# Transposing attention probabilities on VectorE in 32x32 blocks instead of on TensorE

## The chip, the cores and the metric

The kernel runs on one core of a Trainium2 chip. The metric is the device time of one execution in microseconds (us). The core has engines that run beside each other, each through its own list of instructions in order: PE (TensorE, matrix products into PSUM), DVE (VectorE), ACT (ScalarE), POOL (GpSimd, unused here) and SP (SyncE, which here only issues the weight loads). An instruction waits, and everything behind it on its engine waits too, until the instructions of other engines that it depends on have finished.

## The reference

It is a two-layer decoder trunk over 256 tokens of width 2048, with 256 memory tokens. Layer 0 mixes tokens by trailing-window pooling, layer 1 by causal attention with 12 heads of 128; in both, 4 more heads attend to the memory tokens. With one block of 256 tokens the block-sparse attention is plain causal attention. Cut to what matters:

```python
for i in range(2):
    if i == 1: k, v = split(h @ w_kv_shared)               # 12 heads
    branch_in, gate_b, mem_q, gate_m = split(h @ w_in[i])
    branch = multiscale_pool(branch_in) if i == 0 else causal_attention(branch_in, k, v)
    mem_o = softmax(mem_q @ mk.T * 128**-0.5) @ mv         # 4 heads; mk, mv = split(mem @ w_mem_kv[i])
    mixed = concatenate([branch * silu(gate_b), mem_o * silu(gate_m)])
    h = layer_norm(alpha * h + mixed @ w_out[i])
```

Softmax runs over keys. The product with the values needs the probabilities with keys on the partitions, so they have to be transposed.

## The kernel before

Every matrix is streamed through the core in blocks of 128x1024 fp32 numbers (512 KB; `item`). A product is done at about fp32 precision with three products of rounded parts: `split` (L69) copies a block on ACT into a rounded high part (`wh`), and DVE subtracts it from the block to get the low part (`wl`). PE multiplies high by high, high by low and low by high, accumulating in PSUM (`acc`). One block feeds 16 matmuls in `proj_t` or 12 wider ones in `proj_n`.

`run` (L130) writes the order by hand. In the step of block i it emits, in this order, the `split` of block i+3 (`LP = 3`), the DMA load of block i+4 (`LD = 4`, issued by SP), the matmuls of block i (its `consume`), and then the events of step i. An event is a piece of other work that `later(n, fn)` (L92) has put n blocks behind the block at which it was planned. There are four buffers for `wh` and four for `wl` (`W_BUFS = 4`), so the split of block i+3 takes the buffer of block i-1 and can start when PE is through with that one.

Attention is done for two heads at a time: `MemPair` for memory heads, `MobaPair` for the 12 causal ones. Each layer has two memory pairs, layer 1 has six causal pairs (three groups of two): ten pairs in all. A pair has these pieces: `a` (PE computes the scores `s`, DVE the negated row maxima `nb`), `exps` (ACT: exponentials and row sums), `divide` (DVE: reciprocal and four scalings), `b(j)` for each head (PE transposes the probabilities `p` against `ident` into the PSUM tile `pt`, L312 and L362; ACT and DVE split `pt` into `ph`, `pl`), and `c` (PE multiplies by the values into `o`; `gated` multiplies by the gate on DVE and splits the result into `zT`, which the output projection reads). `plan(pr, a, b, c)` (L380) gives the blocks at which `a`, the first `b` and `c` stand, counted from the last query block of the pair's group; `exps` and `divide` stand one and two blocks after `a`, the second `b` one after the first. Below, "block n" is the n-th block after that last query block, and "block 0" is the query block itself.

Of the kernel before, what the change touches and what calls it, by code (L numbers as in the profile page):

```python
# [11 lines left out]
F32 = mybir.dt.float32  # L12
F32R = mybir.dt.float32r
AF = mybir.ActivationFunctionType
ALU = mybir.AluOpType
AX = mybir.AxisListType

P = 128
T = 256
# [13 lines left out]
BLK = 1024  # L33
RAW_BUFS = 4
WARM = 10
SHIFT = 40
W_BUFS = 4
SHIFT = 40
LD = 4
# [6 lines left out]
def trunk(ctx: ExitStack, tc: tile.TileContext, a: dict, out: bass.AP):  # L46
    nc = tc.nc
    ctx.enter_context(tc.manual_schedule())
    sb = ctx.enter_context(tc.tile_pool(name="sb", bufs=1))
    ps = ctx.enter_context(tc.tile_pool(name="ps", bufs=1, space=bass.MemoryType.PSUM))  # L50
# [7 lines left out]
    kept = [xm[:, i * KX:(i + 1) * KX].rearrange("p (k n) -> p k n", k=KT) for i in range(2)]  # L58
    zT = sb.tile([P, KT, 2 * T], F32R, name="zT")
    res = sb.tile([P, 2, D], F32, name="res")  # L60
    ident = mask = psc = eps_t = stats = None

    f = lambda ap: ap.bitcast(F32)

# [4 lines left out]
    def split(hi, lo, src):  # L69

        nc.scalar.activation(hi, src, AF.Copy)  # L71
        nc.vector.tensor_sub(lo, src, f(hi))  # L72
# [19 lines left out]
    def later(n, fn):  # L92
        events[now[0] + n].append(fn)
# [162 lines left out]
    class Rows:  # L256
# [17 lines left out]
        def divide(self):  # L274
            nc.vector.reciprocal(self.sm, self.sm)
            for c, (src, dst) in enumerate(self.rows):
                nc.vector.tensor_scalar_mul(dst, dst, self.sm[:, c:c + 1])

    def gated(o, g, kt):

        zf = sb.tile([P, T], F32, name="zf", bufs=3)
        nc.vector.scalar_tensor_tensor(zf, o, 0.5, g, op0=ALU.mult, op1=ALU.mult)  # L282
        split(zT[:, kt, :T], zT[:, kt, T:], zf)

    class MemPair(Rows):
        def __init__(self, h0, st):
# [2 lines left out]
        def a(self):  # L289
            q, k = self.st["q"], self.st["k"]  # L290
            s = ps.tile([P, 2, 2, T], F32, name="s2")
            for j in range(2):
                h = self.h0 + j
                for t in range(2):
                    qh = q[:, h, t * P:(t + 1) * P]
                    ql = q[:, h, T + t * P:T + (t + 1) * P]
                    mm(s[:, j, t], qh, k[:, h, :T], True, False)
                    mm(s[:, j, t], qh, k[:, h, T:], False, False)
                    mm(s[:, j, t], ql, k[:, h, :T], False, True)
            self.p = p = sb.tile([P, 2, 512], F32, name="p")  # L300
            p4 = p.rearrange("p j (t m) -> p j t m", t=2)
            self.rows = [(s[:, j, t], p4[:, j, t]) for j in range(2) for t in range(2)]
            self.maxima([(0, 4, s)])

        def b(self, j):
            if j == 0:
                self.ph = sb.tile([P, 2, 512], F32R, name="ph")
                self.pl = sb.tile([P, 2, 512], F32R, name="pl")
            pt = ps.tile([P, 512], F32, name="pt")
            for m in range(2):  # L310
                for t in range(2):
                    nc.tensor.transpose(pt[:, m * T + t * P:m * T + (t + 1) * P],  # L312
                                        self.p[:, j, t * T + m * P:t * T + (m + 1) * P], ident)
            split(self.ph[:, j], self.pl[:, j], pt)

        def c(self):
            v, g = self.st["v"], self.st["g"]
            o = ps.tile([P, 2, T], F32, name="o")
            for j in range(2):
                h = self.h0 + j  # L320
                for m in range(2):
                    vh = v[:, m, 0, h * HD:(h + 1) * HD]
                    vl = v[:, m, 1, h * HD:(h + 1) * HD]
                    s = slice(m * T, (m + 1) * T)
                    mm(o[:, j], vh, self.ph[:, j, s], m == 0, False)
                    mm(o[:, j], vh, self.pl[:, j, s], False, False)
                    mm(o[:, j], vl, self.ph[:, j, s], False, m == 1)
            for j in range(2):
                gated(o[:, j], g[:, self.h0 + j, :], 12 + self.h0 + j)

    class MobaPair(Rows):

# [4 lines left out]
        def a(self):  # L337
            q, k = self.st["q"], self.st["k"]
            s = ps.tile([P, 2, 512], F32, name="s2")
            for j in range(2):  # L340
                h = self.h0 + j
                for t, (c0, w) in enumerate(((0, P), (P, T))):
                    qh = q[:, h, t * P:(t + 1) * P]
                    ql = q[:, h, T + t * P:T + (t + 1) * P]
                    d = s[:, j, c0:c0 + w]
                    mm(d, qh, k[:, h, :w], True, False)
                    mm(d, qh, k[:, h, T:T + w], False, False)
                    mm(d, ql, k[:, h, :w], False, True)
            self.p = p = sb.tile([P, 2, 512], F32, name="p")
            nc.vector.tensor_tensor(p[:, :, :384], s[:, :, :384],  # L350
                                    mask[:, None, :].to_broadcast([P, 2, 384]), op=ALU.add)

            self.rows = [(p[:, j, c0:c1],) * 2 for c0, c1 in ((0, P), (P, 384)) for j in range(2)]
            self.maxima([(0, 2, p[:, :, :P]), (2, 4, p[:, :, P:384])])

        def b(self, j):
            if j == 0:
                self.ph = sb.tile([P, 2, 512], F32R, name="ph")
                self.pl = sb.tile([P, 2, 512], F32R, name="pl")
            pt = ps.tile([P, 512], F32, name="pt")  # L360
            for c in range(3):
                nc.tensor.transpose(pt[:, c * P:(c + 1) * P], self.p[:, j, c * P:(c + 1) * P], ident)  # L362
            split(self.ph[:, j, :384], self.pl[:, j, :384], pt[:, :384])

        def c(self):
            v, g = self.st["v"], self.st["g"]
            o = ps.tile([P, 2, T], F32, name="o")
            for j in range(2):
                h = self.h0 + j

                for m, (d, s) in enumerate(((o[:, j], slice(0, T)), (o[:, j, P:], slice(T, 384)))):
                    vh = v[:, m, 0, h * HD:(h + 1) * HD]
                    vl = v[:, m, 1, h * HD:(h + 1) * HD]
                    mm(d, vh, self.ph[:, j, s], m == 0, False)
                    mm(d, vh, self.pl[:, j, s], False, False)
                    mm(d, vl, self.ph[:, j, s], False, m == 1)
            for j in range(2):
                gated(o[:, j], g[:, self.h0 + j, :], self.kt0 + j)

    def plan(pr, a, b, c):  # L380

        later(a, pr.a)
        later(a + 1, pr.exps)
        later(a + 2, pr.divide)
        later(b, lambda: pr.b(0))
        later(b + 1, lambda: pr.b(1))
        later(c, pr.c)
# [21 lines left out]
    def load_gb(n):  # L409
        gb = []  # L410
        for nm in ("ln_g", "ln_b"):
            tl = sb.tile([P, 512], F32, name=nm, bufs=2)
            src = a[nm][0, n * 512:(n + 1) * 512]
            nc.sync.dma_start(tl, src[None, :].to_broadcast([P, 512]))
            gb.append(tl)
        return gb
# [13 lines left out]

    def constants():

        nonlocal ident, mask, psc, eps_t, stats
        ident = sb.tile([P, P], F32, name="ident")
        mask = sb.tile([P, 384], F32, name="mask")
        psc = sb.tile([P, 12], F32, name="psc")
        eps_t = sb.tile([P, 48], F32, name="eps_t")
        stats = sb.tile([P, 2, 5, 6], F32, name="stats")
        nc.vector.memset(eps_t[:, 0:1], EPS)
        nc.scalar.dma_start(ident, a["ident"])  # L440
        nc.scalar.dma_start(mask, a["mask"])
        for g in range(2):
            inv.append(sb.tile([P, 2, T], F32, name="ln_g", bufs=2))
            nc.scalar.dma_start(inv[g], a["inv"][None, 2 * g:2 * g + 2].to_broadcast([P, 2, T]))
        nc.scalar.dma_start(psc, a["pool_scale"])

        def prepare():
            nc.vector.tensor_scalar_mul(psc, psc, 0.5)
            for z in (U0, U1, S0, S1):
                nc.vector.memset(z[:, :, :PAD], 0.0)  # L450
        later(20, prepare)
# [44 lines left out]
    def mem_q_gate(layer):  # L496
        q = fresh("q", lambda: heads_tile("qq"))
        g = fresh("g", gate_tile)
        for c in range(2):
            proj_t(xT, w_in(layer, 12 + c), to_heads(q, 2 * c))  # L500
        prs = [MemPair(0, st), MemPair(2, st)]

        def go():
            plan(prs[0], 1, 5, 9)
            plan(prs[1], 7, 11, 14)
        after(go)
        for c in range(2):
            proj_t(xT, w_in(layer, 14 + c), to_gate(g, 2 * c))
# [98 lines left out]
    for half in range(2):  # L607
# [3 lines left out]
        g = fresh("g", gate_tile)  # L611
# [43 lines left out]
    for grp in range(3):  # L655
        k = fresh("k", lambda: heads_tile("kk"))
        q = fresh("q", lambda: heads_tile("qq"))
        g = fresh("g", gate_tile)
# [5 lines left out]
        prs = [MobaPair(2 * j, 4 * grp + 2 * j, st) for j in range(2)]  # L664

        def go(prs=prs):
            plan(prs[0], 1, 5, 17)
            plan(prs[1], 7, 18, 20)
        after(go)
        for c in range(2):  # L670
            proj_t(xT, w_in(1, 6 + 2 * grp + c), to_gate(g, 2 * c))
# [94 lines left out]
    o = last(0, 0, 512)  # L766
# [95 lines left out]
```

## Time and profile before

| what | value |
|---|---|
| median of 3 runs | 822.19 us (822.07 to 822.66) |
| profiled execution, its own time | 822.53 us |
| its span, first to last instruction | 820.8 us |
| PE busy | 810.8 us, 99% of the span |
| DVE busy | 558.5 us, 68% |
| ACT busy | 396.2 us, 48% |
| HBM traffic | 193 GB/s over the span |

The span is what the trace covers; 1.7 us of the execution's own time lie around it. Busy time of PE counts overlapping matmuls once, so a busy PE says that it had work, not how fast it worked. What a piece of PE's work costs is read from the chain of waits, in which each piece begins where the one before has ended.

### The profile page before, as it was taken

How to read it: one execution, taken by the hardware profiler on the slowest of the kernel's cores; microseconds unless marked ns; L12 is line 12 of the kernel's file. 1: busy time of each engine (PE TensorE's matmuls, PEld its weight loads, DVE VectorE, ACT ScalarE, POOL GpSimd, SP SyncE). 2: the span in 40 equal slices, each digit the busy share in tenths (PEclk: the TensorE clock that was granted, in tenths of full speed). 3: DMA queues.
4: the chain of work that ended last, by engine and by line, in shares of the span. 5: the costliest groups of instructions: out<-in, count | busy, mean ns of one | idle time of the engine just before them, and what ended most of it. 6: DMA issues, size and time to landing. Idle time of an engine off the chain costs nothing.

```text
span 820.8 us, 11537 instructions
## 1 busy us (share of the span) xinstructions
PE 810.8 (99%) x4446; PEld 700.9 (85%) x4446; DVE 558.5 (68%) x794; ACT 396.2 (48%) x578; POOL 0.2 (0%) x4
## 2 busy tenths in 40 slices
PE   9999999999999999999999999999999999999996
PEld 6888888898888888888888888888888888888885
DVE  5786678657956555797667667576765667658746
ACT  6564545545545343545455445354554445545520
POOL 0000000000000000000000000000000000000000
PEclk9999999999999999999999999999999999999998
DMA  8876545456557655676554544645455554636742
GB/s 319 298 250 206 170 154 192 172 181 212 185 190 278 221 186 199 201 234 201 185 170 143 193 162 163 212 159 189 177 173 170 185 187 158 224 113 233 277 132 103
DMA packets 47164, 159.15 MB, mean 194 GB/s; under 512 B 5375, under 2 KB 7167, under 8 KB 46847
## 3 DMA queue, kind: packets, MB, share of 16 engines
q1 hardware_dynamic: 45792, 155.21, 56.3%
q10 hardware_dynamic: 1316, 3.19, 1.0%
q8 instruction: 35, 0.57, 0.3%
q14 instruction: 21, 0.17, 0.1%
HBM read 156.28 MB, written 2.10 MB: 193 GB/s over the span
## 4 chain that ended last, share of the span: by engine, by line
PE 98%; DVE 1%; DMA 1%; SPq 0%; ACT 0%; issue 0%; DVEq 0%
PE acc L67 89%; PE o L67 4%; PE s L67 2%; PE pt L67 2%; DMA raw<-in_w_mk 1%; PE pt L362 0%; PE pt L312 0%; SPq L98 0%; DVE res L805 0%; PE o L637 0%; PE pt L637 0%; DVE res L786 0%; DVE wl L72 0%; ACT wh L71 0%; DVE stats L744 0%
## 5 line engine op out<-in xcount | busy, mean ns | idle before, releaser
L67 PE MATMUL acc<-xm,wh 128*128 128x512 f32 x1344 | 466.8, 394 | 0.5 <-ACT wh L71 0.5
L72 DVE TENSOR_TENSOR wl<-raw,wh 128x1024 fp32r<-128x1024 f32 (+2 forms) x250 | 295.0, 1187 | 149.8 <-ACT wh L71 148.8
L67 PE MATMUL acc<-xm,wl 128*128 128x256 f32 x1344 | 362.6, 280 | 0.1
L71 ACT ACTIVATE wh<-raw 128x1024 fp32r<-128x1024 f32 (+2 forms) x250 | 255.5, 1028 | 188.5 <-PE acc L67 131.2
L67 PEld LDWEIGHTS acc<-xm,wh 128*128 128x128 f32 x1344 | 247.2, 188 | 49.1 <-ACT wh L71 1.0
L67 PEld LDWEIGHTS acc<-xm,wl 128*128 128x128 f32 x1344 | 252.7, 188 | 7.9 <-DVE wl L72 0.9
L67 PE MATMUL acc<-wh,zT 128*128 128x512 f32 x448 | 140.0, 390 | 0.0
L67 PEld LDWEIGHTS acc<-wh,zT 128*128 128x128 f32 x448 | 84.1, 188 | 17.3
L67 PE MATMUL acc<-wl,zT 128*128 128x512 f32 x224 | 87.2, 389 | 0.0
L67 PE MATMUL acc<-xm 128*128 128x512 f32 x288 | 65.8, 389 | 0.0
L67 PEld LDWEIGHTS acc<-xm 128*128 128x128 f32 x288 | 54.1, 188 | 11.2
L72 DVE TENSOR_TENSOR xm<-raw,xm 128x1024 fp32r<-128x1024 f32 (+2 forms) x41 | 47.8, 1171 | 21.1 <-ACT xm L71 21.1
L220 ACT ACTIVATE fold<-acc 128x256 f32<-128x256 f32 x72 | 27.7, 385 | 60.8 <-PE acc L67 59.6
L71 ACT ACTIVATE xm<-raw 128x1024 fp32r<-128x1024 f32 (+2 forms) x41 | 41.3, 1014 | 19.1 <-PE acc L67 9.8
L67 PEld LDWEIGHTS acc<-wl,zT 128*128 128x128 f32 x224 | 42.1, 188 | 8.5
L221 DVE TENSOR_TENSOR fold<-acc,fold 128x256 f32<-128x256 f32 x72 | 29.5, 419 | 4.6 <-ACT fold L220 4.6
L71 ACT ACTIVATE zT<-zf 128x256 fp32r<-128x256 f32 x32 | 12.9, 414 | 39.6 <-DVE zf L282 35.4
L67 PE MATMUL acc<-xm,zT 128*128 128x256 f32 (+1 forms) x144 | 22.6, 318 | 0.0
L67 PEld LDWEIGHTS acc<-xm,zT 128*128 128x128 f32 x144 | 20.7, 190 | 1.9
L67 PE MATMUL acc<-wh,xm 128*128 128x512 f32 x64 | 21.6, 403 | 0.0
L71 ACT ACTIVATE ph<-pt 128x384 fp32r<-128x384 f32 (+1 forms) x20 | 10.7, 535 | 22.2 <-PE pt L362 13.5
L72 DVE TENSOR_TENSOR zT<-zf,zT 128x256 fp32r<-128x256 f32 x32 | 12.9, 423 | 9.7 <-ACT zT L71 9.7
(124 smaller groups left out, 504.4 us busy)
## 6 DMA issues: line engine op xcount, KB each, us to landing
raw<-in_w_in SPq DMA_DIRECT2D x128, 512.0 KB, 3.5
raw<-in_w_out SPq DMA_DIRECT2D x64, 512.0 KB, 4.1
raw<-in_w_sk SPq DMA_DIRECT2D x24, 512.0 KB, 4.4
raw<-in_w_sv SPq DMA_DIRECT2D x24, 512.0 KB, 3.3
raw<-in_w_mv SPq DMA_DIRECT2D x14, 512.0 KB, 5.2
raw<-in_w_mk SPq DMA_DIRECT2D x12, 512.0 KB, 3.4
raw<-in_xT SPq DMA_DIRECT2D x4, 512.0 KB, 4.8
res<-in_x ACTq DMA_DIRECT2D x2, 1024.0 KB, 5.4
```

The source lines that it names most:

```text
L67: nc.tensor.matmul(o, l, r, start=start, stop=stop)
L71: nc.scalar.activation(hi, src, AF.Copy)
L72: nc.vector.tensor_sub(lo, src, f(hi))
L220: nc.scalar.activation(dst, acc[:, T:], AF.Copy)
L221: nc.vector.tensor_add(dst, acc[:, :T], dst)
```

## The change

All 68 transposes on PE go. In their place DVE transposes the divided probabilities in blocks of 32x32 (`turn`): one instruction reads 32 partitions and writes 32 others, transposing each 32x32 block on the way; 16 instructions (four `turn` groups of four) do a pair. For that `exps` writes the exponentials into a new tile `ebuf`, with columns rearranged in pieces of 32, `divide` scales them there, `turn` writes into `p`, and `b` splits `p` instead of `pt`. `ebuf` is one tile for all pairs, and it takes the place of the two `ln_b` buffers of the first layer norm. `gated` does both heads' products first and then both splits. The plans change: the second pair's `a` stands one block later, `turn` groups stand between `divide` and `b`, and the `b` and `c` of memory pairs stand later, the second pair's `c` at block 23 instead of 14.

```diff
+        def blocks(self, n):
+            self.n = 32 * n
+            self.p = sb.tile([P, 2, 512], F32, name="p").rearrange("p j c -> p (j c)")
+            self.e = ebuf.rearrange("p j c -> p (j c)")[:, :4 * self.n]
...
+        def turn(self, *groups):
+            for g in groups:
+                for h in range(4):
+                    nc.vector.transpose(self.p[32 * g:32 * g + 32, h * self.n:(h + 1) * self.n],
+                                        self.e[32 * h:32 * h + 32, g * self.n:(g + 1) * self.n])
...
-        zf = sb.tile([P, T], F32, name="zf", bufs=3)
-        nc.vector.scalar_tensor_tensor(zf, o, 0.5, g, op0=ALU.mult, op1=ALU.mult)
-        split(zT[:, kt, :T], zT[:, kt, T:], zf)
+        zfs = [sb.tile([P, T], F32, name="zf", bufs=3) for _ in range(2)]
+        for j, zf in enumerate(zfs):
+            nc.vector.scalar_tensor_tensor(zf, o[:, j], 0.5, g[:, j], op0=ALU.mult, op1=ALU.mult)
+        for j, zf in enumerate(zfs):
+            split(zT[:, kt + j, :T], zT[:, kt + j, T:], zf)
...
-            pt = ps.tile([P, 512], F32, name="pt")
-            for m in range(2):
-                for t in range(2):
-                    nc.tensor.transpose(pt[:, m * T + t * P:m * T + (t + 1) * P],
-                                        self.p[:, j, t * T + m * P:t * T + (m + 1) * P], ident)
-            split(self.ph[:, j], self.pl[:, j], pt)
+            hi, lo = (t[:, j].rearrange("p (m h s) -> p m h s", m=4, h=4) for t in (self.ph, self.pl))
+            split(hi, lo, self.group(self.p, 4 * j, 4 * j + 4, 4))
...
-    def plan(pr, a, b, c):
+    def plan(pr, a, turns, b, c):
...
+        for g, t in enumerate(turns):
+            later(t, lambda g=g: pr.turn(g))
...
-            tl = sb.tile([P, 512], F32, name=nm, bufs=2)
+            tl = sb.tile([P, 512], F32, name=nm, bufs=2) if nm == "ln_g" else ebuf[:, n % 2]
...
-            plan(prs[0], 1, 5, 9)
-            plan(prs[1], 7, 11, 14)
+            plan(prs[0], 1, (4, 5, 6, 6), 7, 10)
+            plan(prs[1], 8, (11, 13, 16, 18), 20, 23)
...
-            plan(prs[0], 1, 5, 17)
-            plan(prs[1], 7, 18, 20)
+            plan(prs[0], 1, (4, 5, 5, 6), 7, 17)
+            plan(prs[1], 8, (11, 13, 14, 15), 18, 20)
```

The following shows DVE's list in layer 0 from block 14 to block 20 of the memory heads, where the pooling begins (`res` is scratch for the pooling there, its three-part rows are pooling steps of a group of 384 channels). Before:

```order
L282 SCALAR_TENSOR_TENSOR zf<-o,gate 128x256
L72 TENSOR_TENSOR zT<-zf,zT 128x256
L72 TENSOR_TENSOR wl<-raw,wh 128x1024 x2
L221 TENSOR_TENSOR res<-acc,res 128x256 x2
L541 TENSOR_TENSOR res<-res 128x3x256
L72 TENSOR_TENSOR wl<-raw,wh 128x1024
L549 TENSOR_TENSOR res<-res,ln_g 128x3x256
L72 TENSOR_TENSOR wl<-raw,wh 128x1024
L550 TENSOR_TENSOR res<-res 128x3x256
L72 TENSOR_TENSOR zT<-res,zT 128x3x256
L72 TENSOR_TENSOR wl<-raw,wh 128x1024 x2
```

And now:

```order
L294 STREAM_TRANSPOSE p<-ebuf 32x256 x4
L71 TENSOR_TENSOR wl<-raw,wh 128x1024 x3
L220 TENSOR_TENSOR res<-acc,res 128x256 x2
L294 STREAM_TRANSPOSE p<-ebuf 32x256 x4
L559 TENSOR_TENSOR res<-res 128x3x256
L71 TENSOR_TENSOR wl<-raw,wh 128x1024
L567 TENSOR_TENSOR res<-res,ln_g 128x3x256
L71 TENSOR_TENSOR wl<-raw,wh 128x1024
L294 STREAM_TRANSPOSE p<-ebuf 32x256 x4
L568 TENSOR_TENSOR res<-res 128x3x256
L71 TENSOR_TENSOR zT<-res,zT 128x3x256
L71 TENSOR_TENSOR wl<-raw,wh 128x1024 x2
```

Two groups of four transposes (blocks 16 and 18) now stand among the pooling steps, in front of the `wl` of block 22, which is the first of the two in the last row; the second pair's `gated` has left the head of the piece.

On DVE in the first group of causal heads, from block 4 to block 7 of the first pair (`xm` takes the low parts of the value blocks there). Before:

```order
L221 TENSOR_TENSOR fold<-acc,fold 128x256 x2
L72 TENSOR_TENSOR wl<-raw,wh 128x1024
L72 TENSOR_TENSOR pl<-pt,ph 128x384
L242 SCALAR_TENSOR_TENSOR gate<-th,fold 128x256 x2
L72 TENSOR_TENSOR xm<-raw,xm 128x1024
L72 TENSOR_TENSOR pl<-pt,ph 128x384
```

And now:

```order
L220 TENSOR_TENSOR fold<-acc,fold 128x256 x2
L294 STREAM_TRANSPOSE p<-ebuf 32x192 x4
L71 TENSOR_TENSOR wl<-raw,wh 128x1024
L294 STREAM_TRANSPOSE p<-ebuf 32x192 x8
L241 SCALAR_TENSOR_TENSOR gate<-th,fold 128x256 x2
L71 TENSOR_TENSOR xm<-raw,xm 128x1024
L294 STREAM_TRANSPOSE p<-ebuf 32x192 x4
L71 TENSOR_TENSOR xm<-raw,xm 128x1024
L71 TENSOR_TENSOR pl<-p,ph 128x384
```

Sixteen transposes stand within three blocks, and the split of the first head (`pl`) has moved two blocks back behind them.

## Rows read from the trace of the kernel before

**Rows 1.** Page, busy time by engine and granted clock by slice.

```profile
...
PE 810.8 (99%) x4446; PEld 700.9 (85%) x4446; DVE 558.5 (68%) x794; ACT 396.2 (48%) x578; POOL 0.2 (0%) x4
...
PEclk9999999999999999999999999999999999999998
...
```

**Rows 2.** Chain of waits, pieces in order: start us, us, what, matmuls.

```profile
...
88.76 0.44 PE pt L312 x4
89.20 2.78 PE acc L67 x16
...
118.41 1.44 PE o L67 x12
119.85 52.80 PE acc L67 x304
...
496.46 0.33 PE pt L362 x3
...
733.75 76.87 PE acc L67 x384
...
```

**Rows 3.** PE by line and form: count, busy us, mean ns, idle before.

```profile
...
L362 PE MATMUL pt<-ident,p 128*128 128x128 f32 x36 | 5.9, 271 | 0.0
...
L312 PE MATMUL pt<-ident,p 128*128 128x128 f32 x32 | 4.8, 272 | 0.0
...
```

**Rows 4.** Waits: engine and line, waited for, us, times, longest.

```profile
...
ACT wh L71 <- PE acc L67: 131.2, 83, 2.0
...
PE pt L793 <- DVE cc L790: 2.8, 1, 2.8
...
PE acc L67 <- ACT wh L71: 0.5, 1, 0.5
...
```

**Rows 5.** DVE by line and form, columns as in rows 3.

```profile
...
L72 DVE TENSOR_TENSOR wl<-raw,wh 128x1024 fp32r<-128x1024 f32 x234 | 284.7, 1223 | 144.8 <-ACT wh L71 143.9
...
L282 DVE SCALAR_TENSOR_TENSOR zf<-o,gate 128x256 f32<-128x256 f32 x20 | 8.4, 420 | 9.3 <-PE o L67 9.3
L277 DVE TENSOR_SCALAR p<-p,sm 128x256 f32<-128x256 f32 x28 | 8.2, 350 | 0.1
L72 DVE TENSOR_TENSOR pl<-pt,ph 128x384 fp32r<-128x384 f32 x12 | 6.7, 556 | 6.6 <-ACT ph L71 6.6
...
L541 DVE TENSOR_TENSOR res<-res 128x768 f32<-128x768 f32 x10 | 9.5, 954 | 0.1
...
```

**Rows 6.** DVE in order of time, one divide: start us, us, operation, count.

```profile
...
83.46 1.14 DVE L277 TENSOR_SCALAR p<-p,sm 128x256 f32<-128x256 f32 x4
...
```

**Rows 7.** ACT and DVE in order of time, split of block 30, layer 0.

```profile
...
153.17 1.06 ACT L71 ACTIVATE wh<-raw 128x1024 fp32r<-128x1024 f32 x1 [1.71 <-PE acc L67]
...
154.26 1.23 DVE L72 TENSOR_TENSOR wl<-raw,wh 128x1024 fp32r<-128x1024 f32 x1 [1.55 <-ACT wh L71]
```

**Rows 8.** ACT and DVE, the pooling before block 22, layer 0.

```profile
...
130.41 0.95 DVE L550 TENSOR_TENSOR res<-res 128x768 f32<-128x768 f32 x1
...
131.39 0.85 ACT L71 ACTIVATE zT<-res 128x768 fp32r<-128x768 f32 x1 [2.16 <-DVE res L550]
...
132.15 1.05 ACT L71 ACTIVATE wh<-raw 128x1024 fp32r<-128x1024 f32 x1
...
133.22 1.23 DVE L72 TENSOR_TENSOR wl<-raw,wh 128x1024 fp32r<-128x1024 f32 x1
...
```

**Rows 9.** Busy us of engines in three stretches, with PE clock.

```profile
...
core 0: us, PE busy (x) PEld busy (x) DVE busy (x) ACT busy (x) POOL busy (x), PEclk, DMA share, GB/s
76.20:147.60 71.40, 71.40 (x433) 63.63 (x433) 52.01 (x74) 37.64 (x64) 0.00 (x0) 1.00 0.51 170
409.73:484.00 74.27, 74.27 (x451) 66.14 (x450) 50.61 (x83) 38.69 (x66) 0.00 (x0) 1.00 0.52 171
483.95:531.42 47.47, 47.47 (x257) 41.01 (x256) 30.63 (x47) 24.46 (x44) 0.00 (x0) 1.00 0.53 178
...
```

More of the change, by code (lines that the diff above doesn't have):

```diff
@@ L35 @@
 WARM = 10
-SHIFT = 40
 W_BUFS = 4
@@ L60, in trunk @@
     res = sb.tile([P, 2, D], F32, name="res")
-    ident = mask = psc = eps_t = stats = None
+    ident = mask = psc = eps_t = stats = ebuf = None
     f = lambda ap: ap.bitcast(F32)
@@ L277, in divide, with group @@
                 nc.vector.tensor_scalar_mul(dst, dst, self.sm[:, c:c + 1])
-    def gated(o, g, kt):
-        zf = sb.tile([P, T], F32, name="zf", bufs=3)
-        nc.vector.scalar_tensor_tensor(zf, o, 0.5, g, op0=ALU.mult, op1=ALU.mult)
-        split(zT[:, kt, :T], zT[:, kt, T:], zf)
+        def blocks(self, n):
+            self.n = 32 * n
+            self.p = sb.tile([P, 2, 512], F32, name="p").rearrange("p j c -> p (j c)")
+            self.e = ebuf.rearrange("p j c -> p (j c)")[:, :4 * self.n]
+        def group(self, t, c0, c1, m):
+            t = t[:, :4 * self.n].rearrange("p (g x) -> p g x", g=4)[:, :, 32 * c0:32 * c1]
+            return t.rearrange("p g (m s) -> p m g s", m=m)
+        def turn(self, *groups):
[3 more added lines that the diff above has]
+                                        self.e[32 * h:32 * h + 32, g * self.n:(g + 1) * self.n])
+    def gated(o, g, kt):
+        zfs = [sb.tile([P, T], F32, name="zf", bufs=3) for _ in range(2)]
[3 more added lines that the diff above has]
+            split(zT[:, kt + j, :T], zT[:, kt + j, T:], zf)
     class MemPair(Rows):
@@ L299, in a @@
                     mm(s[:, j, t], ql, k[:, h, :T], False, True)
-            self.p = p = sb.tile([P, 2, 512], F32, name="p")
-            p4 = p.rearrange("p j (t m) -> p j t m", t=2)
-            self.rows = [(s[:, j, t], p4[:, j, t]) for j in range(2) for t in range(2)]
+            self.blocks(8)
+            e = self.e.rearrange("p (g j m t s) -> p j t m g s", g=4, j=2, m=2, t=2)
+            self.rows = [(s[:, j, t].rearrange("p (m g s) -> p m g s", m=2, g=4), e[:, j, t])
+                         for j in range(2) for t in range(2)]
             self.maxima([(0, 4, s)])
@@ L327, in c @@
                     mm(o[:, j], vl, self.ph[:, j, s], False, m == 1)
-            for j in range(2):
-                gated(o[:, j], g[:, self.h0 + j, :], 12 + self.h0 + j)
+            gated(o, g[:, self.h0:self.h0 + 2], 12 + self.h0)
     class MobaPair(Rows):
@@ L348, in a @@
                     mm(d, ql, k[:, h, :w], False, True)
-            self.p = p = sb.tile([P, 2, 512], F32, name="p")
+            self.blocks(6)
+            p = self.p.rearrange("p (j c) -> p j c", j=2)
             nc.vector.tensor_tensor(p[:, :, :384], s[:, :, :384],
                                     mask[:, None, :].to_broadcast([P, 2, 384]), op=ALU.add)
-            self.rows = [(p[:, j, c0:c1],) * 2 for c0, c1 in ((0, P), (P, 384)) for j in range(2)]
+            self.rows = [(p[:, j, c0 * P:c1 * P].rearrange("p (m g s) -> p m g s", m=c1 - c0, g=4),
+                          self.group(self.e, 3 * j + c0, 3 * j + c1, c1 - c0))
+                         for c0, c1 in ((0, 1), (1, 3)) for j in range(2)]
             self.maxima([(0, 2, p[:, :, :P]), (2, 4, p[:, :, P:384])])
@@ L359, in b @@
                 self.pl = sb.tile([P, 2, 512], F32R, name="pl")
[L360 to L363, printed above, removed]
+            hi, lo = (t[:, j, :384].rearrange("p (m h s) -> p m h s", m=3, h=4) for t in (self.ph, self.pl))
+            split(hi, lo, self.group(self.p, 3 * j, 3 * j + 3, 3))
         def c(self):
@@ L376, in c @@
                     mm(d, vl, self.ph[:, j, s], False, m == 1)
-            for j in range(2):
-                gated(o[:, j], g[:, self.h0 + j, :], self.kt0 + j)
-    def plan(pr, a, b, c):
+            gated(o, g[:, self.h0:self.h0 + 2], self.kt0)
+    def plan(pr, a, turns, b, c):
         later(a, pr.a)
@@ L431, in constants @@
     def constants():
-        nonlocal ident, mask, psc, eps_t, stats
+        nonlocal ident, mask, psc, eps_t, stats, ebuf
         ident = sb.tile([P, P], F32, name="ident")
@@ L438, in constants @@
         stats = sb.tile([P, 2, 5, 6], F32, name="stats")
+        ebuf = sb.tile([P, 2, 512], F32, name="ebuf")
         nc.vector.memset(eps_t[:, 0:1], EPS)
```

## The prediction

> **What bounds the kernel now.** I read the page first: PE is busy for 810.8 of 820.8 us, DVE for 558.5, ACT for 396.2, and the granted clock stands at 9 tenths or more from the first slice to the last but one [rows 1]. A busy PE may still be waiting inside a stretch, so the waits come next. Few end on PE: the longest takes 2.8 us in the tail after the last product, and for a weight block PE waited once, 0.5 us, while ACT waited 83 times and 131.2 us in total for PE to give back a weight buffer [rows 4]: the other engines run ahead and are held back by PE. The chain of waits says the same: it is one line of PE pieces, each starting where the last ended, up to 733.75 + 76.87 = 810.6 us [rows 2]. A microsecond of work taken off PE is therefore a microsecond of time, as long as DVE and ACT stay ahead; and work given to DVE costs nothing until it makes PE wait.
>
> **What goes from PE.** The transposes of one head stand in the chain as 0.44 us for the four of a memory head and 0.33 us for the three of a causal head; what follows is an ordinary block of 16 matmuls in 2.78 us, so nothing of the price is hidden in the next piece [rows 2]. There are 8 such pieces of memory heads (2 layers with 4 heads) and 12 of causal heads: 8 x 0.44 + 12 x 0.33 = 3.52 + 3.96 = 7.48 us. The products `s` and `o` remain, at other places in PE's list, with the same instructions.
>
> **What comes on DVE.** Ten pairs with 16 transposes each: 64 over 256 columns for the four memory pairs, 96 over 192 for the six causal ones. The trace of before has no such instruction, so its cost is bounded by neighbours. Below: a one-input operation at 256 columns takes 0.35 us [rows 5]. A two-input one takes 0.42 us at 256 columns and 0.556 at 384, a line of 0.136 us for 128 columns, so some 0.35 at 192 [rows 5]. Above: if a transpose went at a quarter of that rate, it would cost what 1024 and 768 columns cost, 1.22 and 0.95 us [rows 5]. Nothing on DVE goes below zero, so there is no gain in this part. I take 0.42 and 0.35, the rows of the same column counts, since the instruction has one pass over its columns like them: 64 x 0.42 + 96 x 0.35 = 60.5 us, and DVE rises from 558.5 to some 619 us. I also take no overlap between them: four scalings of 0.35 that follow each other take 1.14 instead of 1.40 us [rows 6], but all of those use the same 128 partitions, and a transpose reads other partitions than the one in front of it.
>
> [...]
>
> **Is DVE still ahead?** How far it runs ahead: in a quiet stretch ACT starts the split of block 30 at 153.17, just when PE begins block 27, and DVE ends it at 155.49 [rows 7]; PE needs it three blocks after 153.17, at 153.17 + 3 x 2.78 = 161.5. So DVE may fall back by 6 us before PE waits.
>
> First by stage, in the stretches where a pair's pieces lie [rows 9]. Memory heads of layer 0: 71.40 us with 52.01 on DVE leave 19.4 idle, less the 1.76 us by which PE gets shorter there, 17.6; 32 x 0.42 = 13.4 go in. Layer 1: 74.27 - 50.61 - 1.76 = 21.9, again 13.4. A group of causal heads (the first of three that look alike): 47.47 - 30.63 - 0.66 = 16.2 for 32 x 0.35 = 11.2. All three hold the work, the last to 90%.
>
> Then at the tightest place, the start of pooling. Block 14's `o` ends the piece at 119.85 [rows 2], so block 22 starts seven blocks later at 119.85 + 7 x 2.78 = 139.3. Its `wl` ends at 134.45, behind a pooling step, ACT's copy of that and ACT's copy of the block [rows 8]: 4.85 us ahead. The change puts two groups of four transposes (blocks 16 and 18) in front of that step: 8 x 0.42 = 3.4 us later, against a PE that loses as much as the list before it does. That leaves some 1.5 us, and no wait. From there on two `pl` splits stand in the later blocks, but the pooling pauses between its groups. In the causal groups three blocks hold 16 transposes, 5.6 us, beside three `wl`, two folds and two gates (3.7 + 0.8 + 0.8): 10.9 us in 8.3 us, a fall of 2.6 out of 6.
>
> **The rest, with one answer.** `exps` writes in pieces of 32 columns; should that double ACT's 0.5 us, it is 40 x 0.5 = 20 us on an engine at 48%, and two blocks lie between `exps` and the first `turn`. `b` reads SBUF instead of PSUM with the same sizes. The later `c` of the memory pairs delays `zT` rows that the output projection reads a whole pooling or attention stage later. `gated` in its new order takes two waits of DVE on ACT away, off the path. The `ln_b` loads keep their place in SP's queue, and the readers of `ebuf` in layer 0 end at block 20 of the memory heads, before the pooling's second half. If any of these covers failed, the price would again be a wait on `wl`, which the rivals hold.
>
> **Sum.** 822.53 (the profiled execution) - 7.48 = 815.05; the median of before is 0.34 below its profiled execution, so on that footing 814.7. I say 814.9, with 814 to 816 for this case alone.
>
> **Rivals.**
> *DVE is late in places.* At 0.60 us for 256 columns the eight transposes before block 22 eat 1.44 us more and the margin there is gone; at 0.75 (0.63 for 192) PE waits 8 x 0.33 - 1.5 = 1.1 us there, and each causal group, with 32 x 0.63 = 20.2 for 16.2 us of room, uses 4 of its 6 us. Or ACT, which now waits for DVE before `ph`, holds up a `wh` behind it. For: DVE and ACT wait for each other at the pooling [rows 8]. Against: PE waited for them hardly at all so far [rows 4]. Two to seven us come back: 817 to 822.
>
> *DVE becomes the bound: slower.* It is the same place with a dearer transpose. At 1.22 and 0.95 us: layer 0, 39.0 - 17.6 - 6 = 15; layer 1, 39.0 - 21.9 - 6 = 11; causal, (30.4 - 16.2 - 6) x 3 = 25; together 51 against 7.5 gained, about 866. It decides from about 0.87 us for 256 columns (0.72 for 192): 27.8 - 17.6 - 6 = 4.2 and 3 x (23.0 - 16.2 - 6) = 2.4, with the tight place's own wait about the whole gain. For it speaks only that no transpose on DVE is in the trace, against it that every row there costs about 1.06 ns a column or less.
>
> *The gain is larger.* Busy time puts 0.27 us on each transpose [rows 3]; 68 x 0.27 = 18.4 us would give 804. Against: the chain has 0.11 us for each, since matmuls overlap [rows 2]. [...]
>
> **How the numbers follow.** Forecast 0.82, DVE late 0.10, DVE the bound 0.05, larger gain 0.03. A measurement of this kernel can tell some 0.2% (1.6 us) from no change. Forecast, larger gain and 0.07 of "late" lie under 820.5: faster 0.92; the other 0.03 of "late" are the same; slower 0.05. The range goes from 813.6, for what the chain's rounding and another run's start may give, to 818.5, half into "late"; outside lie the two small cases, the upper half of "late" and a few per cent of the forecast.
>
> **What would show it.** Right: no PE piece named `pt` from probabilities, a span near 813.3, PE at 99% with no new wait for `wl` or `ph`, DVE near 619 us, and transposes at 0.35 to 0.45 us. The margin holds if the `wl` before block 22 still ends ahead of PE. Wrong: PE waiting for DVE `wl` or ACT `wh` from 120 us to 150 us or in the causal groups, with transposes above 0.6 us; or a granted clock that falls after such waits.

## The result, and the profile after

The changed kernel takes 814.32 us, median of four runs (814.14 to 814.69), beside 822.27 us for four runs of the kernel before; the ratio is 0.9903 with a 95% interval of 0.9886 to 0.992. The forecast was 814.9, in a range of 813.6 to 818.5.

The page of the changed kernel: span, busy time by engine, and granted clock in 40 slices.

```profile
span 812.9 us, 11568 instructions
...
PE 803.7 (99%) x4378; PEld 694.1 (85%) x4378; DVE 617.4 (76%) x954; ACT 394.1 (48%) x578; POOL 0.2 (0%) x4
...
PEclk9999999999999999999999999999999999999998
...
```

The span is 7.9 us shorter, and PE's busy time 7.1 us. PE still fills 99% of it, at a granted clock of 0.996 in mean. DVE has gone from 558.5 to 617.4 us [rows 1], the forecast's 619.

The chain of waits of the changed kernel (start us, us, what, matmuls):

```profile
...
76.29 1.44 PE s L66 x12
77.73 19.45 PE acc L66 x112
...
105.61 36.12 PE acc L66 x208
141.73 1.44 PE o L66 x12
...
726.09 76.87 PE acc L66 x384
...
```

No piece named `pt` from probabilities is left. Between the scores of the two memory pairs of layer 0 there are now 19.45 us of ordinary blocks (7 x 2.78). The last piece has the same 76.87 us as before and starts at 726.09 instead of 733.75 [rows 2]: 7.66 us earlier, where the sum had 7.48. The remaining 0.2 us lie in the tail behind it.

What PE waited for in the whole trace (waited for, us, times, longest):

```profile
...
PE pt L811 <- DVE cc L808: 2.7, 1, 2.7
PE pt L66 <- DVE zT L124: 1.2, 1, 1.2
PE acc L66 <- ACT cct L813: 0.4, 1, 0.4
```

These are the waits of the start and the tail; none is for `wl`, `wh` or `ph`. The two groups of DVE's new instruction (count, busy us, mean ns, idle before):

```profile
...
L294 DVE STREAM_TRANSPOSE p<-ebuf 32x192 f32<-32x192 f32 x96 | 35.5, 369 | 1.5
...
L294 DVE STREAM_TRANSPOSE p<-ebuf 32x256 f32<-32x256 f32 x64 | 27.9, 436 | 1.0
...
```

One costs 0.436 us at 256 columns and 0.369 at 192, against the 0.42 and 0.35 taken from neighbours [rows 5]; together 63.4 us instead of 60.5.

DVE before block 22 of layer 0, in order of time:

```profile
...
129.14 1.79 DVE L294 STREAM_TRANSPOSE p<-ebuf 32x256 f32<-32x256 f32 x4
130.96 0.96 DVE L568 TENSOR_TENSOR res<-res 128x768 f32<-128x768 f32 x1
132.83 0.96 DVE L71 TENSOR_TENSOR zT<-res,zT 128x768 fp32r<-128x768 f32 x1 [0.91 <-ACT zT L70]
133.78 2.36 DVE L71 TENSOR_TENSOR wl<-raw,wh 128x1024 fp32r<-128x1024 f32 x2
```

Four transposes take 1.79 us, 0.45 each, with a mean of 0.436 for one, so they do not overlap; four scalings do (1.14 us for four of 0.35, [rows 6]). The forecast's reason, that each transpose reads other partitions than the one in front of it, was its author's estimate; no run tests it. The last row holds the `wl` of blocks 22 and 23; the first of them ends near 135.0. Block 22 starts two blocks before 141.73, at 136.17. The margin is 1.2 us, where the forecast had 1.5 and the kernel before 4.85.

### The profile page after: what moved, and what is told of

Read it like the earlier page. It is cut to its first block, busy times and chain, and to the rows that moved or that the text cites. A ratio compares the mean times of both kernels' runs of the same rounds, so it can differ in the third digit from the quotient of the medians.

```text
span 812.9 us, 11568 instructions
## 1 busy us (share of the span) xinstructions
PE 803.7 (99%) x4378; PEld 694.1 (85%) x4378; DVE 617.4 (76%) x954; ACT 394.1 (48%) x578; POOL 0.2 (0%) x4
## 4 chain that ended last, share of the span: by engine, by line
PE 99%; DVE 1%; issue 0%; DVEq 0%; ACT 0%
PE acc L66 90%; PE o L66 4%; PE pt L66 2%; PE s L66 2%; DVE res L823 0%; PE pt L655 0%; PE o L655 0%; DVE res L804 0%; DVE stats L762 0%; DVE res L761 0%; DVEq L876 0%; PE pt L811 0%; DVE mv L800 0%; DVE zT L124 0%; ACT cct L813 0%
## 5 line engine op out<-in xcount | busy, mean ns | idle before, releaser
L294 DVE STREAM_TRANSPOSE p<-ebuf 32x192 f32<-32x192 f32 (+1 forms) x160 | 63.4, 396 | 2.4
L70 ACT ACTIVATE ph<-p 128x384 fp32r<-128x384 f32 (+1 forms) x20 | 11.2, 561 | 29.1 <-DVE p L294 29.1
L66 PE MATMUL acc<-xm,zT 128*128 128x256 f32 (+1 forms) x144 | 22.6, 318 | 0.0
```

The lines of the kernel that those rows point to most:

```text
L66: nc.tensor.matmul(o, l, r, start=start, stop=stop)
L294: nc.vector.transpose(self.p[32 * g:32 * g + 32, h * self.n:(h + 1) * self.n], self.e[32 * h:32 * h + 32, g * self.n:(g + 1) * self.n])
```

## Experiments

The theory: what counts is PE's own time for the transposes, and DVE's work is hidden as long as DVE does not fall too far behind PE. The rivals: part of the gain comes from the new order, or from waits on PE's transposes that ACT and DVE no longer have; and, for the limit of the change, whether a dearer or denser run of transposes is paid from the room of a whole stretch or where it stands. The first four runs were timed beside before at 822.38 us, the next four beside 822.35 and the last three beside 822.08.

**Order alone.** In the kernel before, with the transposes on PE and the new order in `gated`:

```diff
...
-            plan(prs[0], 1, 5, 9)
-            plan(prs[1], 7, 11, 14)
+            plan(prs[0], 1, 7, 10)
+            plan(prs[1], 8, 20, 23)
...
-            plan(prs[0], 1, 5, 17)
-            plan(prs[1], 7, 18, 20)
+            plan(prs[0], 1, 7, 17)
+            plan(prs[1], 8, 18, 20)
```

> The kernel before with the plan's blocks for a, b and c and the order inside gated of the changed kernel; the transposes stay on PE. If the gain is PE's own time for the transposes, 822.3 us within 1 us, as before. If the later places of b and c or the new order of gated bring part of the gain, 820 us or less; if they bring all of it, 814 to 815 us.

822.15 us, ratio 0.9997 (0.9988 to 1.0006): the places of `b` and `c` and the order in `gated` bring nothing. PE's pieces stand in the chain at their new places with their old price:

```profile
...
94.34 0.44 PE pt L314 x4
...
502.00 0.33 PE pt L363 x3
...
```

**PE's transposes put back beside DVE's.** In `b` of the changed kernel, four for a memory head and three for a causal one:

```diff
+            pt = ps.tile([P, 512], F32, name="pt")
+            for c in range(4):
+                nc.tensor.transpose(pt[:, c * P:(c + 1) * P], f(xT[:, c, :P]), ident)
             split(hi, lo, self.group(self.p, 4 * j, 4 * j + 4, 4))
...
```

> The changed kernel in which PE also does as many 128x128 transposes as before at the places of b, of a tile that is ready and into a PSUM tile that nobody reads. If the gain is PE's own time, 8 x 0.44 + 12 x 0.35 = 7.7 us come back: 822.0 us (821.3 to 822.8), with the 0.44 and 0.33 us pieces in the chain. If PE had room for them, or if what had cost was the wait of ACT and DVE for PE's transposes, 814 to 817 us.

821.89 us, ratio 0.9995 (0.9986 to 1.0005). Nothing waits for these transposes and nothing reads them, and yet 7.6 us are back:

```profile
...
94.05 0.44 PE pt L333 x4
...
501.77 0.33 PE pt L384 x3
...
```

The gain is PE's own time, and no wait of ACT or DVE had a part in it.

**No transposes on DVE.** The changed kernel without `turn`, `b` reading the scaled exponentials as they are:

```diff
-        for g, t in enumerate(turns):
-            later(t, lambda g=g: pr.turn(g))
...
-            split(hi, lo, self.group(self.p, 4 * j, 4 * j + 4, 4))
+            split(hi, lo, self.group(self.e, 4 * j, 4 * j + 4, 4))
...
```

> The changed kernel without any transpose: b splits the scaled exponentials as they are (left out: the transposition, so the attention is of untransposed probabilities). DVE's 63.4 us go. If this work is wholly hidden, 814.3 us within 0.8 us and the same PE chain; if the transposes on DVE cost PE something in small waits or a lower clock, 812 us or less.

814.51 us (814.35 to 814.58), the changed kernel's 814.32 within the spread of the runs. Its page:

```profile
span 812.8 us, 11408 instructions
...
PE 803.6 (99%) x4378; PEld 694.0 (85%) x4378; DVE 557.6 (69%) x794; ACT 395.7 (49%) x578; POOL 0.2 (0%) x4
...
```

DVE does 60 us less and the span is the same: the work put on DVE costs nothing.

**Every transpose twice.** `for g in groups * 2` in `turn`.

> Every transpose on DVE is done twice in place, so each stands for one of 0.87 us at 256 columns and 0.74 at 192. Theory (a lead of 6 us, room by stage): layer 0 gets 14.1 us more for 3.7 us of room, less 6 is 4.4; layer 1 14.1 for 8.0, less 6 is 0; each causal group 11.8 for 4.4, less 6 is 1.4, three times; together 8.6, so 823 us (819 to 827), with PE waiting for wl or wh from 125 to 150 us. If DVE has much more room than the ledger says: 814 to 816 us. If one wait drags the next through ACT: above 830 us.

887.23 us, ratio 1.0792 (1.0774 to 1.081): 73 us slower than the changed kernel, far above the 823 of the ledger. Its page, and what PE waited for:

```profile
...
PE 825.4 (93%) x4378; PEld 703.7 (79%) x4378; DVE 681.0 (77%) x1114; ACT 393.0 (44%) x578; POOL 0.2 (0%) x4
...
```

```profile
...
PE o L66 <- DVE vv L71: 19.5, 3, 6.5
PE acc L66 <- DVE wl L71: 15.0, 7, 5.4
PE acc L66 <- DVE xm L71: 13.0, 15, 1.5
PE acc L66 <- ACT wh L70: 2.9, 1, 2.9
...
```

The new waits are 50.4 us, and PE's busy time is 21.7 us higher for the same matmuls: 72.1 of the 72.4 us by which the span grew. DVE is busy for 77% only, so it is not short of time in all; it is late at certain places.

**The old plan.** The transposes on DVE, but all 16 of a pair at one block, with the old places of `a`, `b` and `c`:

```diff
-            plan(prs[0], 1, (4, 5, 6, 6), 7, 10)
-            plan(prs[1], 8, (11, 13, 16, 18), 20, 23)
+            plan(prs[0], 1, (4, 4, 4, 4), 5, 9)
+            plan(prs[1], 7, (10, 10, 10, 10), 11, 14)
...
-            plan(prs[0], 1, (4, 5, 5, 6), 7, 17)
-            plan(prs[1], 8, (11, 13, 14, 15), 18, 20)
+            plan(prs[0], 1, (4, 4, 4, 4), 5, 17)
+            plan(prs[1], 7, (10, 10, 10, 10), 18, 20)
```

> The transposes on DVE with the plan of the kernel before: all 16 of a pair at one block, a block before the first b, and the old places of a, b and c. Theory: a burst of 7.0 us with a wl and two gates in a block of 2.8 us makes DVE fall back by about 6.2 us of the 6 it has, at the four memory pairs; a causal pair falls back by 5.1 us: 814.3 to 817 us. If spreading them is what makes the change work, each memory pair makes PE wait 3 us or more, in c or for wl: 824 us or more. If the spreading buys nothing at all: 814.3 us, without a wait on PE.

838.65 us, ratio 1.0201 (1.0186 to 1.0216). Here the theory's own number, 814 to 817, was far off. The second memory pair of layer 0, on DVE and then on PE (idle time before a row and its releaser in brackets), and the stretch behind the wait, with the granted clock as the eighth number from the left, behind POOL's:

```profile
...
110.28 7.18 DVE L294 STREAM_TRANSPOSE p<-ebuf 32x256 f32<-32x256 f32 x16
117.49 1.23 DVE L71 TENSOR_TENSOR wl<-raw,wh 128x1024 fp32r<-128x1024 f32 x1
...
```

```profile
...
114.57 0.40 PE L66 MATMUL acc<-xm,wh 128*128 128x512 f32 x1
118.77 0.39 PE L66 MATMUL acc<-xm,wl 128*128 128x256 f32 x1 [3.80 <-DVE wl L71]
...
119.74 0.63 PE L66 MATMUL acc<-xm,wh 128*128 128x512 f32 x1
```

```profile
...
118.80:122.20 3.40, 3.40 (x13) 2.93 (x14) 3.40 (x6) 3.23 (x6) 0.00 (x0) 0.62 0.63 181
...
```

The burst of 7.18 us starts when PE needs the next low part in 4.7 us, not in 8: DVE comes late to this place, and the chain of waits runs back from here to the first pair's burst. PE waits 3.80 us. A matmul of 512 columns then grows from 0.40 to 0.63 us, and the granted clock of the next 3.4 us is 0.62 in mean, where it was 1.00 in the stretch of the wait. The other four second pairs wait 4.24, 2.26, 2.27 and 2.26 us. The span grew by 24.0 us: 15.3 of waits and 8.7 more busy on PE.

**First pairs gathered.** `(4, 4, 4, 4)` for the first pairs alone:

> The changed kernel with the four turn groups of each first pair at one block (4), the second pairs' spread as they are. Theory (DVE may fall back by some 6 us, and only a burst beyond that is felt): a burst of 7.1 us for memory pairs against the 6.3 us that the first pair of the old plan had, 0 to 0.9 us of wait in two places, none in the causal groups: 814.3 to 818 us. If every gathered burst costs 2 us or more, as for the second pairs of the old plan, 824 us or more.

817.27 us (816.84 to 817.61), ratio 0.9938 (0.9923 to 0.9953). DVE and PE in layer 0:

```profile
...
86.85 7.17 DVE L294 STREAM_TRANSPOSE p<-ebuf 32x256 f32<-32x256 f32 x16
94.06 1.23 DVE L71 TENSOR_TENSOR wl<-raw,wh 128x1024 fp32r<-128x1024 f32 x1
...
```

```profile
...
95.34 0.39 PE L66 MATMUL acc<-xm,wl 128*128 128x256 f32 x1 [0.71 <-DVE wl L71]
...
```

A burst on a DVE that is fully ahead costs the 0.7 us that the ledger gave it here, and 1.55 us in layer 1; the causal groups do not wait.

**Second pairs gathered.** `(11, 11, 11, 11)` for the second pairs alone, `b` and `c` late as in the change:

> The changed kernel with the four turn groups of each second pair at one block (11), b and c late as they are. Theory: the second pairs of the old plan made PE wait five times (3.8, 4.2 and three times 2.3 us) because the burst meets a DVE that is already behind, and each wait is followed by up to 3.4 us at half the clock; the late b and c do not change that: 830 to 840 us. If it was the early b and c that made PE wait, 814 to 817 us.

832.8 us (831.38 to 833.94), ratio 1.0124 (1.0107 to 1.0141). What PE waited for:

```profile
...
PE acc L66 <- DVE wl L71: 7.0, 2, 3.9
PE acc L66 <- DVE xm L71: 5.4, 3, 1.8
...
```

The same five places wait, though `b` and `c` stand late. In layer 0 the burst starts at 111.43 and PE needs the next low part at 116.79, in 5.4 us: DVE comes late to this place with the first pair's transposes spread as well. The change lives on the spreading of the second pairs' transposes; the later last steps, which make room for it, do not help by themselves.

**Half more.** Six transposes in each group, `for h in (0, 1, 2, 3, 0, 1)`:

> Six transposes in each turn group instead of four, two of them repeated, as if one cost 0.65 us at 256 columns and 0.55 at 192. The ledger on record (room of a whole stretch plus 6 us): a wait of 0.6 us before block 22 and nothing else, 815 us. The ledger by bursts (three blocks against 6 us): 7.2 us behind in the first memory pairs, 6.7 in the causal groups, 0.6 over at the pooling, so waits of 1.2 twice, 0.7 three times and 0.6: 5.1 us, and up to 1.7 us more for each that brings half the clock: 819 to 826 us.

852.34 us (850.59 to 852.61), ratio 1.036 (1.0345 to 1.0375): both ledgers fail. Its page, and what PE waited for:

```profile
...
PE 818.7 (96%) x4378; PEld 700.2 (82%) x4378; DVE 649.3 (76%) x1034; ACT 393.5 (46%) x578; POOL 0.2 (0%) x4
...
```

```profile
...
PE o L66 <- DVE vv L71: 12.4, 3, 4.2
PE acc L66 <- DVE wl L71: 6.8, 9, 1.6
...
PE acc L66 <- DVE xm L71: 2.0, 4, 0.6
PE acc L66 <- ACT wh L70: 1.4, 1, 1.4
...
```

More than half of the waiting, 12.4 of 22.6 us, is in a place that neither ledger had: the products `o` of the first causal pair waiting for `vv`, the low part of the values. The stretch of the first such wait, and the one behind it:

```profile
...
541.90:546.10 4.20, 0.09 (x1) 0.00 (x0) 4.03 (x9) 0.00 (x0) 0.00 (x0) 0.82 0.38 125
546.10:552.50 6.40, 6.38 (x26) 5.78 (x27) 4.90 (x8) 2.11 (x4) 0.00 (x0) 0.58 0.52 166
...
```

PE does nothing for some 4 us; then the granted clock is 0.58 in mean for 6.4 us. PE's busy time is 15.0 us above the changed kernel's; with the waits that makes 37.6 of 37.9 us.

In the changed kernel DVE stands at this place like this:

```profile
...
523.16 1.53 DVE L294 STREAM_TRANSPOSE p<-ebuf 32x192 f32<-32x192 f32 x4
524.72 1.22 DVE L71 TENSOR_TENSOR wl<-raw,wh 128x1024 fp32r<-128x1024 f32 x1
525.86 1.28 DVE L71 TENSOR_TENSOR vv<-acc,vv 128x512 fp32r<-128x512 f32 x2
...
```

The last `turn` group, a `wl`, and the two low parts of the values, which end at 527.14, while PE begins the products at 527.10 and comes to the low parts some 0.2 to 0.5 us later (the first of the two ends near 526.5, and the first product that needs it starts at 527.33). Three runs test this.

**One group more before the values.** In the causal second pairs, `(11, 13, 14, 15, 15)` with `pr.turn(g % 4)`:

> The changed kernel with one turn group of each causal second pair done once more at block 15: 1.5 us more on DVE in front of the low part of the values, which the products of block 17 need 0.5 us after it is ready. Theory (this is the tightest place): PE waits 0.7 to 1.0 us in each of three groups, 816.5 to 817.5 us, up to 824 us if half the clock follows each wait. If DVE has the 6 us there that it has for weight blocks, 814.3 us.

818.39 us (818.01 to 819.09), ratio 0.9955 (0.994 to 0.997). DVE, and then PE at the wait:

```profile
...
523.02 3.12 DVE L294 STREAM_TRANSPOSE p<-ebuf 32x192 f32<-32x192 f32 x8
...
527.32 1.28 DVE L71 TENSOR_TENSOR vv<-acc,vv 128x512 fp32r<-128x512 f32 x2
...
```

```profile
...
528.05 0.44 PE L66 MATMUL o<-ph,vv 128*128 128x256 f32 x2 [0.76 <-DVE vv L71]
...
```

Three waits of 0.76 to 0.77 us, for 1.53 us more on DVE: the margin of the changed kernel is 0.8 us there. The span of the profiled execution is 3.3 us longer than the changed kernel's: 2.3 are these waits, 0.6 is in PE's busy time, and 0.4 is not placed (the medians differ by 4.1 us).

**One group more at the pooling.** In the memory second pairs, `(11, 13, 16, 18, 18)`:

> The changed kernel with one turn group of each memory second pair done once more at block 18: 1.8 us more on DVE in front of the low part of block 22, which is 1.2 us ahead of PE in layer 0. Theory: a wait of 0.6 us in layer 0 and none in layer 1, 814.9 us (814.4 to 815.5; 816.6 with half the clock behind it). If the pooling were as tight as the causal groups, or ACT dragged more behind it, 817 us or more.

815.12 us (814.82 to 815.45), ratio 0.9914 (0.99 to 0.9929), with one wait there:

```profile
...
136.94 0.38 PE L66 MATMUL acc<-xm,wl 128*128 128x256 f32 x1 [0.42 <-DVE wl L71]
...
```

1.8 us more make PE wait 0.42 us, so the margin before block 22 is 1.4 us by this run.

**Half more, and the products a block later.** As the run with half more, with the causal first pairs' `c` at 18 instead of 17:

> Six transposes in each turn group as in the run with half more (852.3 us), and the products of each causal first pair one block later, at 18. Theory: three of its waits, 4.1 us each, were for the low part of the values in front of these products; with a block of 2.8 us between, 1.3 us of each is left and less of the half clock behind them (6.8 us spells before): 834 to 842 us. If DVE is simply over its work in these groups, so that a later place only moves the wait, 850 to 853 us.

839.35 us (837.12 to 843.16), ratio 1.02 (1.0182 to 1.0218).

```profile
...
PE acc L66 <- DVE wl L71: 7.0, 10, 1.6
PE o L66 <- DVE vv L71: 3.6, 3, 1.2
...
```

The wait for `vv` falls from 12.4 to 3.6 us, and the span by 9.4: a wait, not DVE's total, was what cost there. The span is still 28.5 us above the changed kernel's: 14.0 us of waits, none longer than 1.6, and 14.0 us more busy on PE. Behind each of the three waits for `vv`, of 1.20 to 1.24 us, matmuls of 512 columns take some 0.63 us for a stretch instead of 0.39; the first wait, and the stretch behind it, at a granted clock of 0.50 in mean:

```profile
...
546.41 0.45 PE L66 MATMUL o<-ph,vv 128*128 128x256 f32 x2 [1.21 <-DVE vv L71]
...
548.00:551.40 3.40, 3.40 (x12) 2.90 (x12) 3.19 (x7) 1.81 (x4) 0.00 (x0) 0.50 0.73 230
...
```

The four executions take 837.12 to 843.16 us at a mean granted clock of 0.995 down to 0.988, and the profiled one is the slowest: how much the clock costs differs here from one execution to the next.

## Why the prediction was right

**PE's price.** Taken from the chain, 0.44 and 0.33 us a piece, it gave 7.48 us; measured are 7.66 up to the last piece, 7.6 when the transposes were put back, and nothing for the order alone. The busy durations, which would have given 18.4, were no price.

**DVE's price.** 0.42 and 0.35 from the rows of the same column counts were 0.436 and 0.369, and no overlap was right. Between the two, 64 columns cost 67 ns, 1.05 ns a column, as the slope of the neighbours had it. That DVE's total came out within 2 us of the forecast's 619 is in part luck: the transposes took 2.9 us more than the sum gave them, and the busy time of DVE's other work fell by 4.5 us. The run without them shows that all 63.4 us are hidden. By stage, DVE was busy for 59.73 of 67.70 us in layer 0 and 42.15 of 46.70 us in the first causal group:

```profile
...
core 0: us, PE busy (x) PEld busy (x) DVE busy (x) ACT busy (x) POOL busy (x), PEclk, DMA share, GB/s
76.30:144.00 67.70, 67.70 (x406) 60.17 (x406) 59.73 (x99) 33.96 (x59) 0.00 (x0) 1.00 0.51 167
480.50:527.20 46.70, 46.70 (x249) 40.25 (x249) 42.15 (x80) 24.21 (x44) 0.00 (x0) 1.00 0.55 175
...
```

The forecast had 90% for the latter; it is 90%. ACT's waits on DVE, up to 6.4 us before `ph`, are new and cost nothing, as the plan leaves `ph` time before `c`.

**The margin.** 1.5 us before block 22 was 1.2 by the trace and 1.4 by its experiment (the low part is needed by the block's second matmul, 0.2 us behind its start). But that is not the tightest place, as the forecast had it. The step that failed is "DVE may fall back by 6 us before PE waits", applied to everything PE needs from DVE. It holds for weight blocks, which are split three blocks ahead. The low part of the values can be made only after block 16 and is needed right behind block 17, one block of 2.8 us later, and it stands in DVE's list behind the transposes; its margin is 0.8 us. The prediction did not work this margin out; that the change stayed inside it was luck. (A small slip without effect: the last reader of `ebuf` in layer 0 is the `turn` at block 18, not block 20.)

**The rival "DVE becomes the bound".** Its direction was right and its price wrong. It was to decide from about 0.87 us for 256 columns, and "late in places" at 0.60 to 0.75 us was to cost 2 to 7 us. Transposes of 0.65 us in effect cost 38 us and of 0.87 us 73 us; the kernel is slower than before at 0.65 already. Three terms were missing: room was counted over a whole stretch, where a burst must be paid in the few blocks around it (the old plan, with no more work on DVE, costs 24 us); the products that wait for the values; and the growth of PE's busy time behind waits, 8.7 us in the old plan, 15.0 with half more and 21.7 with each transpose twice. Not all of that is the clock, by an estimate from the mean granted clocks of the profiled executions, 0.987, 0.983 and 0.976 beside the changed kernel's 0.996: the missing share times the span (836.9, 850.8 and 885.3 us, beside 812.9) is 7.6, 11.2 and 18.0 us more than in the changed kernel, PE's waits counted in; the rest is not placed. The forecast named a falling clock as a sign, but put no price on it. At the measured 0.436 us none of this comes in.

## What to carry to other kernels

Where one engine's chain has no gaps, taking work from it is worth what the chain, not the busy time, has for that work (here 7.66 us, not 18.4), and the work may go to an engine that has 10% to spare with it in that stage (here DVE, busy for 42.15 of 46.70 us in the first causal group), if it is laid out so that the chain never waits. Look for the margin at each thing the chain takes from that engine, above all at what can be made only one step before it is needed; slack over a stretch does not pay for a burst. A place that costs nothing with 0.8 us to spare cost 12.4 us of waits, and more behind them, when the work in front of it grew by half.

## What the runs showed of the hardware that was not expected

In these runs a short wait of PE could cost more than its length. Behind waits of 3.8 to 4.1 us the granted clock was 0.58 to 0.62 in the next 3.4 to 6.4 us, and the same 4378 matmuls kept PE busy for 812.4 us (old plan), 818.7 (half more) and 825.4 (twice) instead of 803.7, at a mean granted clock of 0.987, 0.983 and 0.976 instead of 0.996.

The length of the wait does not decide by itself whether the clock falls. With half more and the products a block later, matmuls of 512 columns took some 0.63 us behind each of three waits of 1.20 to 1.24 us, the first at a granted clock of 0.50, and 0.39 to 0.40 us behind a wait of 1.59 us in layer 1 of the same execution. Behind three waits of 0.76 to 0.77 us (one group more before the values) they took 0.39 to 0.45 us, beside 0.39 to 0.44 at the first of these places in the changed kernel, and behind one of 0.42 us (one group more at the pooling) 0.39 to 0.40. What does decide is open.
